# Encoder block on one core: output projection on two scaled fp16 planes, totals and turns beside the score tiles

## The chip, the cores and the metric

The kernel runs on one core of one Trainium2 chip. A core has five engines that the text speaks of: TensorE (PE in the profile, with its weight loads as PEld), VectorE (DVE), ScalarE (ACT), GpSimd (POOL) and SyncE (SP), whose queue issues DMAs. Each works through its own queue in order, and semaphores hold an instruction until its operands are there. The metric is the device time of one execution in microseconds. Three runs of the kernel before gave 1240.5, 1242.0 and 1242.54, median 1242.0.

## What is computed

The reference, cut to its skeleton (one sequence of 1024 tokens, width 1024, 8 neighbourhood heads, 8 window heads on 2 key/value heads, FF width 4096, all float32):

```
h = layer_norm(x, ln0_g, ln0_b)
proj = h @ w_in + b_in
qa, ka, va, qb, kb, vb, ga, gb = split(proj)
y_na = neighbourhood_attention(qa, ka, va, na_rpb) @ w_branch_na
y_swa = windowed_gqa_with_sink(rotary(qb), rotary(kb), vb, sink) @ w_branch_swa
mixed = sigmoid(ga) * y_na + sigmoid(gb) * y_swa
h = layer_norm(ALPHA * h + mixed @ w_out + b_out, ln1_g, ln1_b)
u = square(relu(h @ w_ff1 + b_ff1))
h = layer_norm(ALPHA * h + u @ w_ff2 + b_ff2, ln2_g, ln2_b)
```

## The kernel before

Products are made on split operands: a float32 matrix is held as a high and a low plane, and three matmuls (high·high, high·low, low·high) stand for one. Most products use fp16 planes, scaled by a power of a mean square so that they fit fp16; the scale goes out again when the result is taken from PSUM. The output projection alone uses float32 planes in the matmul's rounded form (fp32r): there is no scale, the planes are a cast and a subtraction.

**Attention** (up to about 400 us) goes in 64 steps, four per head, each with a pair of score tiles: one in the PSUM tag s, one in t (lines 768 to 771). VectorE takes scores out with the bias and the row's extremum (L772), ScalarE makes exponentials, TensorE multiplies with the values (L878). Between these matmuls stand pieces of the input projection (L420), put there by a filler. Some sums with ones (totals over the partitions, for scales of later operands, L193 and the like) and the turned reciprocals of the softmax sums (L828) are made between steps, each in a PSUM tile of tag t of its own. Near the end of attention three additions of 128x2048 (L1074) form a combined operand for the gate products. Gate weights are loaded in steps 24 and on.

**Gate products** follow (to about 465 us); their results go to memory and are read back as sg, the arguments of the sigmoids.

**Branch products** (about 465 to 551 us): for each of 8 column blocks f and 2 halves of the tokens, `branch` makes 12 fp16 matmuls for the neighbourhood branch in tag t and 12 for the window branch in tag o; VectorE takes each out times scale times sigmoid (L1468), and POOL adds the two into mx (L1470). Around them stand per block: the load of a branch weight, its squares on ScalarE (L1360), its product with ones on TensorE (L1365) and its split (L1375, L1376); the load of a row block of w_out and its cast and subtraction (L1458, L1459). The order is written out by hand, engine by engine, in the loop over f and half; a small table B_AT does this for the first blocks during the gate products.

**Output projection** (551 to 646 us): for each of 8 token groups g, `out_mm` makes 2 x 24 matmuls over the column halves (in tags that alternate between mm and s), `split_mx` makes the two planes of the next group's mx, `out_evac` adds the residual (L1560) and takes the statistics (L1563), `ln1_norm` normalises (POOL L1569, ScalarE L275), `turn` transposes the rows of the group before (L1580) in the middle of the group's second half, `turn_evac` scales these into mx (L1591, L1588), and `combine` makes the planes for the first feed-forward product (L1596, L1597). POOL meanwhile prepares the residual rows of later groups (L1732). This order, too, is written by hand. The feed-forward products follow to the end.

## Time and profile before

| what | value |
|---|---|
| median of three runs | 1242.0 us |
| profiled execution | 1243.25 us |
| its span | 1241.5 us |
| TensorE busy | 1216.2 us, 98% |
| VectorE busy | 966.4 us, 78% |
| ScalarE busy | 850.9 us, 69% |
| POOL busy | 333.6 us, 27% |
| mean granted TensorE clock | 0.996 |

A row of the timeline reads: start, duration, engine, line, operation, output and inputs by the program's names, shapes, count of equal instructions in a row, and in brackets how long the engine stood idle before it and for whom. Matmuls overlap in the array, so the time that one takes is read from start to start and not from its duration.

### The profile page before, as it was taken

The page shows a single profiled execution, that of the slowest core. Times are in us where ns is not written, and L with a number is a line of the kernel's source. Part 1 is how long each engine was busy: PE and PEld are TensorE (multiplying, and loading weights), DVE is VectorE, ACT ScalarE, POOL GpSimd, SP SyncE. Part 2 cuts the span into 40 slices and gives each one's busy share as a digit, 9 for nine tenths or more (in the row PEclk, how much of TensorE's full clock was granted, in tenths as well). Part 3 has the DMA queues.
Part 4 walks back from the last instruction along what each step waited for, and adds up shares of the span by engine and source line. Part 5 has one row for each costly group of instructions (what it writes and reads, how often), then busy time and mean ns, then how long its engine had stood idle before and what let it go on. Part 6 is the DMA issues. An engine that isn't in the chain of part 4 may idle for free.

```text
span 1241.5 us, 17090 instructions
## 1 busy us (share of the span) xinstructions
PE 1216.2 (98%) x6050; PEld 638.4 (51%) x6050; DVE 966.4 (78%) x1401; ACT 850.9 (69%) x1369; POOL 333.6 (27%) x358
## 2 busy tenths in 40 slices
PE   8999999999999999999999999999999999999997
PEld 5546565555555444458874444444444444444443
DVE  6788998878876974555788887877767778898898
ACT  7569889998866466533568877788776846344447
POOL 5202222433430013537620031432300001211207
PEclk9999999999999999999999999999999999999998
DMA  8655668686565336645333456776636636363333
GB/s 318 199 183 116 154 155 181 164 186 157 145 135 154 116 119 215 198 152 207 119 136 119 160 191 235 255 245 230 212 118 243 219 136 229 127 261 128 125 111 135
DMA packets 177877, 216.83 MB, mean 175 GB/s; under 512 B 111744, under 2 KB 125312, under 8 KB 171136
## 3 DMA queue, kind: packets, MB, share of 16 engines
q1 hardware_dynamic: 176816, 214.89, 54.5%
q8 instruction: 47, 0.77, 0.3%
q10 hardware_dynamic: 976, 0.87, 0.2%
q14 instruction: 38, 0.31, 0.1%
HBM read 130.69 MB, written 59.33 MB: 153 GB/s over the span
## 4 chain that ended last, share of the span: by engine, by line
PE 78%; ACT 8%; DVE 7%; DMA 2%; issue 2%; POOL 1%; SPq 0%; ACTq 0%; POOLq 0%; DVEq 0%
PE ps_mm L420 16%; PE ps_t L1719 6%; PE ps_o L1719 6%; PE ps_mm L2193 6%; PE ps_s L2193 6%; PE ps_mm L1719 6%; PE ps_t L2193 5%; PE ps_o L2193 5%; PE ps_s L1719 3%; PE ps_o L878 2%; PE ps_o L1162 2%; PE ps_t L1162 1%; PE ps_mm L1162 1%; PE ps_t L410 1%; PE ps_o L410 1%
## 5 line engine op out<-in xcount | busy, mean ns | idle before, releaser
L420 PE MATMUL ps_mm<-hT 128*128 128x512 f16 x960 | 228.1, 381 | 4.9 <-DVE hT L389 2.0
L1719 PEld LDWEIGHTS <-tw 128*128 128x128 f16 x1248 | 122.0, 99 | 146.1 <-issue 1.9
L2193 PEld LDWEIGHTS <-hS 128*128 128x128 f16 x1008 | 98.6, 98 | 118.2
L420 PEld LDWEIGHTS <-hT 128*128 128x128 f16 x960 | 91.0, 100 | 103.7 <-issue 14.4
L791 ACT ACTIVATE ss<-ss,sk 128x384 f32<-128x384 f32 (+1 forms) x128 | 73.9, 578 | 27.9 <-DVE sk L772 27.8
L1719 PE MATMUL ps_t<-hS,tw 128*128 128x512 f16 x384 | 88.1, 379 | 1.5 <-ACT sn L1819 1.1
L1909 DVE TENSOR_TENSOR usl<-usl 128x512 f32<-128x512 f32 x64 | 52.3, 817 | 23.5 <-ACT usl L1837 23.3
L420 PE MATMUL ps_mm<-hT,wpair 128*128 128x512 f16 x288 | 68.7, 380 | 0.0
L1640 POOL TENSOR_TENSOR c<-c 128x2 f32<-128x2 f32 x16 | 15.5, 976 | 193.8 <-DVE c L1639 193.8
L2213 POOL TENSOR_TENSOR acc<-acc,rst 128x512 f32<-128x512 f32 x16 | 32.2, 2012 | 123.6 <-DMA rst<-xr_d 115.7
L200 POOL TENSOR_TENSOR hT<-hT 128x2 f32<-128x2 f32 x30 | 26.4, 880 | 115.7 <-DVE hT L199 115.7
L2026 DVE SCALAR_TENSOR_TENSOR hS<-stg,c,hS 128x2048 f16<-128x2048 f32 x21 | 51.0, 2429 | 7.6 <-ACT hS L2023 7.6
L1646 DVE SCALAR_TENSOR_TENSOR tw<-raw,c,tw 128x512 f16<-128x512 f32 x60 | 51.1, 852 | 4.2 <-ACT tw L1643 3.9
L2193 PEld LDWEIGHTS <-hA 128*128 128x128 f16 x336 | 32.9, 98 | 39.6
L1162 PEld LDWEIGHTS <-hT 128*128 128x128 f16 x336 | 32.9, 98 | 38.8 <-issue 0.3
L878 PE MATMUL ps_o<-pt,vv 128*128 128x256 f16 (+1 forms) x448 | 49.2, 250 | 1.8 <-DMA pt<-hT 1.8
L803 DVE SCALAR_TENSOR_TENSOR pl<-ss,pl 128x768 f16<-128x768 f32 (+1 forms) x42 | 46.7, 1112 | 1.8 <-ACT pl L794 1.6
L1470 POOL TENSOR_TENSOR mx<-sg 128x512 f32<-128x512 f32 x16 | 32.5, 2031 | 51.6 <-DVE sg L1468 51.6
L878 PEld LDWEIGHTS <-vv 128*128 128x128 f16 x448 | 35.5, 98 | 18.8 <-issue 2.1
L1719 PE MATMUL ps_o<-hS,tw 128*128 128x512 f16 x192 | 44.1, 379 | 0.0
L1643 ACT ACTIVATE tw<-raw,c 128x512 f16<-128x512 f32 x60 | 41.7, 709 | 2.8 <-DVE raw L1684 2.8
L2193 PE MATMUL ps_mm<-hA,hS 128*128 128x512 f16 x192 | 42.9, 379 | 0.0
(413 smaller groups left out, 3066.4 us busy)
## 6 DMA issues: line engine op xcount, KB each, us to landing
us_d<-usl SPq DMA_DIRECT2D x112, 256.0 KB, 3.1
stg<-us_d SPq DMA_DIRECT2D x28, 1024.0 KB, 4.8
raw<-in_w_ff SPq DMA_DIRECT2D x24, 512.0 KB, 5.6
sg<-sg_d SPq DMA_DIRECT2D x32, 256.0 KB, 2.9
hA<-in_w_ff SPq DMA_DIRECT2D x8, 1024.0 KB, 7.7
hS<-in_w_ff SPq DMA_DIRECT2D x8, 1024.0 KB, 7.7
hT<-in_w_in SPq DMA_DIRECT2D x60, 128.0 KB, 2.6
hT<-in_w_in SPq DMA_DIRECT2D x11, 512.0 KB, 4.4
```

What stands on the lines that cost most here:

```text
L420: PE.matmul(ps, a[:, k, :], act(b, k), start=(k == 0 and i == 0), stop=(k == NK - 1 and i == 2))
L791: ACT.activation(p, p, AF.Exp, bias=nm[:, i:i + 1], scale=-1.0, accum_out=sums_l[o_chunk][:, hh, 2 * t + i:2 * t + i + 1])
L803: DVE.scalar_tensor_tensor(out=pl[:, n:2 * n], in0=e[:, 0:n], scalar=P_SCALE, in1=pl[:, 0:n], op0=ALU.mult, op1=ALU.subtract)
L878: PE.matmul(o, vs, move(part), start=(m == 0 and part == 0), stop=(m == len(runs) - 1 and part == 1))
L1162: PE.matmul(ps, w[:, a, k, :], act[:, b, k, :], start=(first and k == 0 and m == 0), stop=(k == 3 and m == 2), skip_group_check=True)
L1470: POOL.tensor_tensor(out=mx[:, f, half * 512:(half + 1) * 512], in0=both[0], in1=both[1], op=ALU.add)
L1643: ACT.activation(hi_lo(slot, 0), src, AF.Copy, bias=0.0, scale=w_scale(p))
L1646: DVE.scalar_tensor_tensor(out=hi_lo(slot, 1), in0=src, scalar=w_scale(p), in1=hi_lo(slot, 0), op0=ALU.mult, op1=ALU.subtract)
L1719: PE.matmul(ps, ww, act[:, part, k, :], start=(first and k == 0 and m == 0), stop=(k == 3 and m == 2), skip_group_check=True)
L1909: DVE.tensor_tensor(out=out, in0=a, in1=b, op=op)
L2026: DVE.scalar_tensor_tensor(out=slot[:, :, 1, :], in0=src, scalar=scale, in1=slot[:, :, 0, :], op0=ALU.mult, op1=ALU.subtract)
L2193: PE.matmul(ps, st[:, a, part, j * P:(j + 1) * P], w[:, a, wpart, :], start=(first and a == 0 and m == 0), stop=(a == 3 and m == 2), skip_ ...
```

## The change

Four things are edited.

1. In the attention steps the totals with ones no longer take a tile of tag t. They are written into columns 384 and up of the newest score tile in tag s, which scores never use; the turned reciprocals go to columns 384 to 511 of the score tile in tag t.
2. The three large additions become six of half the size, one a step; the gate loads come two steps later; one small bound is moved from the last steps of attention to the start of the gate products.
3. The output projection works on scaled fp16 planes. Each row block of w_out gets squares (ScalarE), a product with ones (TensorE), a scale (VectorE, POOL) and a scaled split. mx gets squares per block and half, one scale for tokens 0 to 511, made in the middle of the last branch product, and one for tokens 512 to 1023, made behind group 1 of the projection. The result is scaled back in `out_evac`; the scale of w_out's block goes into the branch's own scale.
4. With that, loads, squares and splits of the branch stage change places, and the split of groups 0 and 1 goes behind the last branch product.

```
-                    self.ps = psum("t") if ps is None else ps
+                    self.ps = total_bank() if ps is None else ps
...
+    def total_bank():
+        if not in_steps:
+            return psum("t")
+        c = 384 + 2 * (n_tot[0] % 64)
+        n_tot[0] += 1
+        return score_ps[0][:, c:c + 2]
...
-            ps = psum("t")
+            ps = score_ps[1][:, 384:512]
...
-                if 6 <= H < 13:
-                    g_load(H - 6, i)
+                q = 4 * H + i - 26
+                if 0 <= q < 28:
+                    g_load(q // 4, q % 4)
...
-                        s1_sum(i - 1)
+                elif 0 <= 4 * H + i - 57 < 6:
+                    s1_sum(4 * H + i - 57)
...
+        def wo_square(k):
+            ACT.activation(junkb, wo_raw[k], AF.Square, accum_out=wsq_o[:, k:k + 1], saturate=False)
+        def wo_scale(k):
+            ps, t = psum("s"), wt_o[:, 2 * k:2 * k + 2]
+            PE.matmul(ps[:, 0:2], ones_b, wsq_o[:, k:k + 1].to_broadcast([P, 2]), start=True, stop=True)
+            DVE.scalar_tensor_tensor(out=t, in0=ps[:, 0:2], scalar=Q_MIN, in1=cvb, op0=ALU.max, op1=ALU.mult)
+            w, b = wsc_o[:, 2 * k:2 * k + 2], bsc[:, 4 * k:4 * k + 4]
+            POOL.tensor_tensor(out=w, in0=t, in1=pwb, op=ALU.pow)
+            POOL.tensor_scalar(out=b[:, 2:4], in0=o_back, scalar1=b[:, 1:2], scalar2=w[:, 1:2],
+                               op0=ALU.mult, op1=ALU.mult)
...
-            ACT.copy(wo[:, 0, k, :], wo_raw[k])
-            DVE.tensor_tensor(out=wo[:, 1, k, :], in0=wo_raw[k], in1=b32(wo[:, 0, k, :]), op=ALU.subtract)
+            ACT.activation(wo[:, 0, k, :], wo_raw[k], AF.Copy, bias=0.0, scale=sc)
+            DVE.scalar_tensor_tensor(out=wo[:, 1, k, :], in0=wo_raw[k], scalar=sc, in1=wo[:, 0, k, :],
+                                     op0=ALU.mult, op1=ALU.subtract)
...
+        def mx_square(f, half):
+            j = 8 * half + f
+            ACT.activation(junkm, mx[:, f, half * 512:(half + 1) * 512], AF.Square, accum_out=msq[:, j:j + 1],
+                           saturate=False)
+        def mx_scale(half, ps, ones_, pw_):
+            DVE.tensor_reduce(out=mtot[:, half:half + 1], in_=msq[:, 8 * half:8 * half + 8], axis=mybir.AxisListType.X,
+                              op=ALU.add)
+            PE.matmul(ps[:, 0:2], ones_, mtot[:, half:half + 1].to_broadcast([P, 2]), start=True, stop=True)
...
-            ACT.copy(m[:, 0], mx[:, :, tok(g)])
-            DVE.tensor_tensor(out=m[:, 1], in0=mx[:, :, tok(g)], in1=b32(m[:, 0]), op=ALU.subtract)
+            ACT.activation(m[:, 0], mx[:, :, tok(g)], AF.Copy, bias=0.0, scale=mx_sc(g, 0))
+            DVE.scalar_tensor_tensor(out=m[:, 1], in0=mx[:, :, tok(g)], scalar=mx_sc(g, 0), in1=m[:, 0],
+                                     op0=ALU.mult, op1=ALU.subtract)
...
+                    if f + 1 < 8:
+                        wo_scale(f + 1)
+                        if f:
+                            b_split(f + 1)
...
+                if half == 0:
+                    if f + 1 < 8:
+                        wo_square(f + 1)
+                    if f + 2 < 8:
+                        b_square(f + 2)
+                if f or half:
+                    mx_square(*((f, 0) if half else (f - 1, 1)))
+                branch(f, half, (lambda: mx_scale(0, psum("s"), ones_b, pwb)) if (f, half) == (7, 1) else None)
...
-                if f == 7 and half == 0:
-                    split_mx(0)
-                    split_mx(1)
+        split_mx(0)
+        split_mx(1)
+        mx_square(7, 1)
...
-        DVE.tensor_tensor(out=z[:, ns], in0=pss[g, n], in1=z[:, ns], op=ALU.add)
+        DVE.scalar_tensor_tensor(out=z[:, ns], in0=pss[g, n], scalar=mx_sc(g, 1), in1=z[:, ns],
+                                 op0=ALU.mult, op1=ALU.add)
...
+            if g == 1:
+                mx_scale(1, psum("o"), ones, pw)
```

The queue of TensorE at the change from the first to the second half of branch 0, before: the window product in ps_o, then the next neighbourhood product in ps_t.

```order
L411 LDWEIGHTS wb
L411 MATMUL ps_o<-oS,wb 128x512
L412 LDWEIGHTS wb
L412 MATMUL ps_o<-oS,wb 128x512
L410 LDWEIGHTS wb
L410 MATMUL ps_t<-oS,wb 128x512
L411 LDWEIGHTS wb
```

The same place now (lines 410 to 412 have become 419 to 421):

```order
L420 LDWEIGHTS wb
L420 MATMUL ps_o<-oS,wb 128x512
L421 LDWEIGHTS wb
L421 MATMUL ps_o<-oS,wb 128x512
L1400 MATMUL ps_s<-bc 128x2
L419 LDWEIGHTS wb
L419 MATMUL ps_t<-oS,wb 128x512
```

A product with ones (L1400, of `wo_scale`) has come between the halves; it reads the squares of the next row block of w_out.

The queue of ScalarE from the first sigmoids (L1449) on, before; L1360 are squares of a branch weight, L1458 the cast of w_out's block.

```order
L1375 ACTIVATE wb<-braw,bc 128x1024
L1449 ACT_TABLE_LOAD
L1449 ACTIVATE sg<-sg,prm 128x512 x6
L1360 ACTIVATE bc<-braw 128x1024
L1458 CAST wo<-raw 128x1024
```

And now (sigmoids L1508, split of w_out's block L1409, its squares L1396, squares of the branch weight L1374, squares of mx L1476):

```order
L1388 ACTIVATE wb<-braw,bc 128x1024
L1508 ACT_TABLE_LOAD
L1508 ACTIVATE sg<-sg,prm 128x512 x2
L1409 ACTIVATE wo<-raw,bc 128x1024
L1508 ACTIVATE sg<-sg,prm 128x512 x2
L1396 ACTIVATE bc<-raw 128x1024
L1374 ACTIVATE bc<-braw 128x1024
L1508 ACTIVATE sg<-sg,prm 128x512 x2
```

The branch weight's squares have moved ahead of the third pair of sigmoids, and the squares of w_out's block, which L1400 reads, stand behind the second pair.

VectorE from the last-but-one branch product to the first projection result, before:

```order
L1459 TENSOR_TENSOR wo<-raw,wo 128x1024
L1468 SCALAR_TENSOR_TENSOR sg<-ps_t,bc,sg 128x512
L1468 SCALAR_TENSOR_TENSOR sg<-ps_o,bc,sg 128x512
L1437 TENSOR_TENSOR m<-mx,m 128x1024 x2
L1468 SCALAR_TENSOR_TENSOR sg<-ps_t,bc,sg 128x512
L1468 SCALAR_TENSOR_TENSOR sg<-ps_o,bc,sg 128x512
L1459 TENSOR_TENSOR wo<-raw,wo 128x1024
L1560 TENSOR_TENSOR z<-ps_mm,z 128x512
```

And now (L1521 takes out a branch product, L1480 and L1484 belong to `mx_scale`, L1495 is the low plane, L1619 the projection's result):

```order
L1521 SCALAR_TENSOR_TENSOR sg<-ps_t,bc,sg 128x512
L1521 SCALAR_TENSOR_TENSOR sg<-ps_o,bc,sg 128x512
L1480 TENSOR_REDUCE prm<-prm 128x1
L1484 TENSOR_SCALAR mxc<-ps_s 128x2
L1521 SCALAR_TENSOR_TENSOR sg<-ps_t,bc,sg 128x512
L1521 SCALAR_TENSOR_TENSOR sg<-ps_o,bc,sg 128x512
L1495 SCALAR_TENSOR_TENSOR m<-mx,mxc,m 128x1024 x2
L1619 SCALAR_TENSOR_TENSOR z<-ps_mm,mxc,z 128x512
```

The low planes of groups 0 and 1 stood ahead of the last branch product's two results and now stand behind both; the sum for the scale stands ahead of them.

## The prediction

> **What bounds the kernel now.** I read the page first, then the chain of waits of TensorE, then the windows and the timeline of the stages that the change touches.

> ```profile
> PE 1216.2 (98%) x6050; PEld 638.4 (51%) x6050; DVE 966.4 (78%) x1401; ACT 850.9 (69%) x1369; POOL 333.6 (27%) x358
> ```

> TensorE is busy 98% of the span; all its idle time is about 25 us. So the change can gain in three ways: shorter matmuls, idle gaps that close, or a clock that is not lowered. It loses wherever a matmul is put in TensorE's queue ahead of work that was ready, with an operand that comes late. The waits of TensorE, with total, count and longest, show the gaps that this change touches:

> ```profile
> PE ps_s L1365 <- ACT bc L1360: 2.1, 1, 2.1
> PE ps_t L770 <- DVE sk L772: 1.6, 3, 1.0
> PE ps_mm L420 <- DVE hT L256: 0.9, 2, 0.7
> PE ps_t L770 <- ACT rt L830: 0.7, 1, 0.7
> PE ps_t L1580 <- ACT z L275: 0.2, 1, 0.2
> ```

> Attention owns the second to fourth, the start of the branch products the first, and the end of the output projection the last. In the projection itself TensorE hardly waits.

> **Attention: totals and turns beside the score tiles.** The gaps at L770 are waits for a free ps_t tile, which the totals with ones (L193) and the turned reciprocals (L828) also took. With those in the score tiles, this wait goes. But a total written into the ps_s score tile must wait until VectorE has evacuated that tile (L772), which it did not before. TensorE, then VectorE, around 141 us:

> ```profile
> 140.74 0.28 PE L193 MATMUL ps_t<-hT 128*128 128x2 f32 x2
> 142.59 0.44 PE L770 MATMUL ps_t<-kh,q 128*128 128x384 f32 x1 [0.33 <-DVE sk L772]
> ```
> ```profile
> 141.37 0.61 DVE L772 CUSTOM_DVE_ANT_0 ss<-ps_s,bd,snk 128x384 f32<-128x384 f32 x1
> ```

> The total stood at 140.74; now it waits for the evacuation to end at 141.98, so everything behind it moves 1.24 us, while the wait at 142.59 (0.33 idle, some 0.48 by starts) goes: +0.76. The step at 173 has the same picture (its total some 1.25 before the evacuation's end): together +1.5. One step gains, since its wait for the evacuated reciprocal goes, −0.75:

> ```profile
> 191.08 0.44 PE L770 MATMUL ps_t<-kh,q 128*128 128x384 f32 x1 [0.75 <-ACT rt L830]
> ```

> Around 358 VectorE is late because of a 2.54-us addition, which the change halves. VectorE, TensorE, and the windows of the stage (the last three columns are the granted clock, the share of the DMA engines and GB/s):

> ```profile
> 356.29 2.54 DVE L1074 TENSOR_TENSOR g<-hT 128x2048 f32<-128x2048 f16 x1
> ```
> ```profile
> 359.83 0.38 PE L770 MATMUL ps_t<-kh,q 128*128 128x256 f32 x1 [0.98 <-DVE sk L772]
> 361.03 4.17 PE L420 MATMUL ps_mm<-hT 128*128 128x512 f16 x11 [0.70 <-DVE hT L256]
> ```
> ```profile
> 360.00:362.00 2.00, 1.30 (x5) 0.55 (x6) 2.00 (x4) 1.94 (x5) 0.01 (x1) 0.73 0.43 153
> 362.00:364.00 2.00, 2.00 (x7) 0.62 (x6) 2.00 (x1) 1.27 (x2) 2.00 (x1) 0.50 0.52 119
> ```

> Two gaps of 0.98 and 0.70 are followed by half clock (0.50), in which 11 matmuls take 4.17 us. With an addition of some 1.27 in place of 2.54 the evacuation comes 1.27 earlier and both gaps nearly close; I leave 0.4 for totals that now wait there: −1.3. If the gaps go, so does the low clock: the 11 matmuls take 11 × 0.216 = 2.4 (0.216 is shown below) instead of 4.1 from start to start, −1.7. Sum of attention: +1.5 − 0.75 − 1.3 − 1.7 = **−2.25**. Unknown is at how many further steps the total now waits; bounds: −3.75 if the two steps cost nothing, 0 if the low clock stays or three more steps cost 0.76. The gate loads, two steps later, lie on the SP queue behind the same neighbours and have steps to spare: 0.

> **Start of the branch products.** TensorE, then ScalarE:

> ```profile
> 470.06 0.38 PE L410 MATMUL ps_t<-oS,wb 128*128 128x512 f16 x1
> ```
> ```profile
> 471.67 1.96 ACT L1449 ACTIVATE sg<-sg,prm 128x512 f32<-128x512 f32 x3 [1.27 <-DMA sg<-sg_d]
> 476.33 1.04 ACT L1360 ACTIVATE bc<-braw 128x1024 fp8e5<-128x1024 f32 x1
> 477.28 0.18 ACT L1360 ACTIVATION_READ_ACCUMULATOR bc<-braw 128x1 f32 x1
> ```

> Before, the squares of a branch weight (L1360) stood behind six sigmoids that wait for DMA, and TensorE waited 2.1 for them, some 2.2 by starts. Now these squares come after only two late sigmoids, and that wait goes. But the product with ones that scales the next output weight stands ahead of the second half of branch 0, ready at 470.06. Its squares (like L1360, 1.04 + 0.18) stand behind two sigmoids whose data land at 471.67: 471.67 + 2 × 0.65 + 1.2 = 474.2. TensorE waits 4.15 instead of 2.2: **+1.95**. VectorE, POOL and the evacuation queue behind it with slack.

> The trace shows what idle time can do to the clock: 1.7 us of it in two gaps was followed by half clock, worth 1.7. A gap of 4.15 in one piece I expect to bring the same: **+1.75**. Against it stands this window, in which a gap of 2.1 left the clock at 1.00:

> ```profile
> 476.00:478.00 2.00, 0.48 (x4) 0.37 (x5) 0.25 (x1) 2.00 (x4) 1.27 (x1) 1.00 0.36 137
> ```

> The bounds are 0 and 2.4.

> Later branches: per f ScalarE has four sigmoids, two splits, two squares of 1024 and two of 512, worked out from these groups as 4 × 0.67 + 2 × 1.15 + 2 × 1.23 + 2 × 0.87 = 9.2 (a 512 square costed like a sigmoid plus its read), within 48 matmuls of 0.216 = 10.4:

> ```profile
> L1449 ACT ACTIVATE sg<-sg,prm 128x512 f32<-128x512 f32 x16 | 10.9, 716 | 10.3 <-DMA sg<-sg_d 10.2
> L1375 ACT ACTIVATE wb<-braw,bc 128x1024 f16<-128x1024 f32 x7 | 8.0, 1148 | 7.4 <-POOL bc L1368 7.4
> ```

> It fits: 0, at most +1.5 where a load is late.

> **End of the branch products and output projection.** POOL, TensorE and VectorE:

> ```profile
> 546.81 1.27 POOL L1470 TENSOR_TENSOR mx<-sg 128x512 f32<-128x512 f32 x1 [3.01 <-DVE sg L1468]
> 548.37 0.38 PE L410 MATMUL ps_o<-oS,wb 128*128 128x512 f16 x1
> 550.31 0.38 PE L410 MATMUL ps_o<-oS,wb 128*128 128x512 f16 x1
> 550.74 0.38 PE L412 MATMUL ps_o<-oS,wb 128*128 128x512 f16 x1
> 551.42 0.39 PE L1553 MATMUL ps_mm<-wo,m 128*128 128x512 f32 x1
> ```

> The scale of the activations needs a sum in the middle of the last branch: the addition ends at 548.08, ScalarE squares 0.87, VectorE reduces some 0.2, so the product with ones starts at about 549.3 where TensorE would go on at 548.37: +0.95. Then the low plane of the first group stands on VectorE behind the evacuation of the last branch tile: 550.74 + 0.95 + 0.43 to the evacuation, 0.67, and a low plane of 1.28 (as L1376):

> ```profile
> 467.88 1.28 DVE L1376 SCALAR_TENSOR_TENSOR wb<-braw,bc,wb 128x1024 f16<-128x1024 f32 x1
> ```

> That gives 554.1 for the third matmul of the projection, which stood at 551.42: +2.7.

> fp16 itself gains. Nine fp16 matmuls take 550.31 − 548.37 = 1.94, 0.216 each; nine of the projection 576.19 − 574.15 = 2.04, 0.227 each:

> ```profile
> 574.15 0.39 PE L1552 MATMUL ps_mm<-wo,m 128*128 128x512 f32 x1
> 576.19 0.39 PE L1552 MATMUL ps_mm<-wo,m 128*128 128x512 f32 x1
> ```

> For 384 matmuls that is −4.3. By the end of group 1 it has given back 94 × 0.011 = 1.0, which leaves +1.65. There the second scale stands ahead of group 2, behind VectorE's work on group 1, which is ready only at 575.97:

> ```profile
> 575.82 0.15 DVE L1568 TENSOR_SCALAR mv<-mv 128x1 f32<-128x1 f32 x1
> 576.96 8.29 POOL L1732 TENSOR_TENSOR zl<-zl 128x512 f32<-128x512 f32 x5
> 590.15 1.25 ACT L275 ACTIVATE zl<-zl,mv 128x1024 f32<-128x1024 f32 x1 [3.32 <-POOL mv L273]
> ```
> ```profile
> L1368 POOL TENSOR_TENSOR bc<-bc 128x2 f32<-128x2 f32 x6 | 4.2, 708 | 2.2 <-DVE bc L1366 2.2
> ```

> With a reduction of 0.2 (the small operation here takes 0.15) TensorE stands some 2.2 more. But from here TensorE is not alone on the path: POOL runs without a gap from 576.96 to the normalisation at 590.15, and its new power (0.7, as the last row, a group of the branch products) goes ahead of that. So z of group 2 comes at +1.65 + 0.7 = +2.4. From then VectorE, POOL and ScalarE go round in a loop:

> ```profile
> 591.93 3.06 DVE L1597 TENSOR_TENSOR hA<-mx,hA 128x512 f16<-128x512 f32 x2 [4.08 <-ACT hA L1596]
> 603.82 3.05 DVE L1597 TENSOR_TENSOR hA<-mx,hA 128x512 f16<-128x512 f32 x2 [2.88 <-ACT hA L1596]
> 640.40 1.23 ACT L275 ACTIVATE z<-z,mv 128x1024 f32<-128x1024 f32 x1
> 641.68 1.09 PE L1580 MATMUL ps_t<-ident,z 128*128 128x128 f32 x8
> ```

> ```profile
> L1468 DVE SCALAR_TENSOR_TENSOR sg<-ps_t,bc,sg 128x512 f32<-128x512 f32 x15 | 11.3, 751 | 12.0 <-PE ps_t L412 5.6 <-issue 4.9 <-POOL bc L1368 0.9
> 599.11 0.68 DVE L1560 TENSOR_TENSOR zl<-ps_s,zl 128x512 f32<-128x512 f32 x1
> ```

> A round takes 11.89, and VectorE's only gap in it, 2.88, waits on ScalarE, not on TensorE. Scaled evacuations (0.75 for 0.68, twice, by the rows here) and low planes (1.28 above, at most 0.05 over a subtraction of that size) add some 0.17 a round, five times. At group 6 z ends at 641.63 and the turn starts at 641.68: no slack. So the end comes at 2.4 + 0.85 = **+3.25** against before, and TensorE spends its saving waiting for turns. Bounds: 2.7 + 2.2 − 4.3 = +0.6 if TensorE alone sets the pace, and +4.

> **Sum.** −2.25 + 1.95 + 1.75 + 3.25 = +4.7. The profiled execution took 1243.25, span 1241.5; the changed one would take 1247.95. It stood 1.25 above the median of 1242.0, so the median becomes 1246.7. A measurement tells 0.2%, 2.5 us, from no change.

> **Rivals.**
> - The clock stays up at the branch start: +2.95, 1245.0. [...] By the trace, gaps of 1.7 in pieces were enough once, and 2.1 not enough once. Chance 0.15.
> - The loop of VectorE, POOL and ScalarE doesn't bind: the turns find their rows ready, the end comes at +0.6 instead of +3.25: +2.05, 1244.05. For it: only 0.2 us of waiting at L1580 is seen. Against: the turn at 641.68 has no slack. Chance 0.20.
> - Not slower: the fp16 saving of 4.3 arrives whole, because the sums for the scales and the first low plane are ready in time at both ends of the projection. −2.25 + 3.7 − 4.3 = −2.85, 1239.15. It decides if VectorE's reductions are done before TensorE gets to the product, which needs some 0.95 and 2.2 that I do not see. That fp16 runs no faster here speaks against this too, but the rows above have it at 0.216. Chance 0.13.
> - Attention costs more: totals wait 0.76 at six more steps, +4.5 on top, 1251.2. Against: VectorE mostly evacuates well before the total. Chance 0.12.

> **The numbers.** My forecast has 0.40, mostly within 1.5 of 1246.7. Slower: 0.36 of it, 0.09 of the first rival, 0.04 of the second, all 0.12 of the last: 0.61. Within 0.2%: 0.04 + 0.06 + 0.14 = 0.24. Faster: 0.02 of the second and 0.13 of the third: 0.15. The range from 1239.5 to 1250.5 leaves out most of the third and the last.

> **What would show it.** Right: a TensorE wait of about 4 us near 470 behind squares on ScalarE, then half clock; waits near 549, at the third projection matmul, and before group 2; matmuls 0.216 apart in the projection; turns waiting for z of groups 5 to 7; 0.98 and 0.70 near 360 gone. Wrong: sigmoid data that land earlier than 4 us after their issue, a round of the loop that shrinks under 11.4, or totals that wait at many steps.

## The result, and the profile after

The changed kernel took 1251.36 us (median; 1251.06 to 1251.82), before 1241.76; ratio 1.0079, 95% interval 1.0061 to 1.0096. It is slower by 9.6 us. The forecast was slower, 1246.7 with a range to 1250.5: the sign was right, the size half of what came, and the measured time lies 0.9 beyond the range.

The profiled execution took 1251.06, span 1249.2. Its page, and TensorE's waits (total, times, longest):

```profile
PE 1215.4 (97%) x6070; PEld 607.5 (49%) x6070; DVE 970.9 (78%) x1416; ACT 870.9 (70%) x1417; POOL 339.2 (27%) x368
```
```profile
PE ps_s L1400 <- ACT bc L1396: 4.3, 1, 4.3
PE ps_s L193 <- DVE sk L781: 2.8, 3, 1.2
PE ps_t L1640 <- ACT z L284: 2.1, 1, 2.1
PE ps_o L1482 <- DVE prm L1480: 2.1, 1, 2.1
...
PE ps_mm L1612 <- DVE m L1495: 1.6, 1, 1.6
...
PE ps_mm L1174 <- DVE go L1249: 0.8, 1, 0.8
...
PE ps_s L1482 <- DVE prm L1480: 0.5, 1, 0.5
```

TensorE is as busy as before (1215.4 for 1216.2), though the projection's matmuls are shorter: what they save went into 20 more matmul instructions for the products with ones (6070 for 6050) and into matmuls at a lower clock. Each wait that the forecast named is there: the squares of w_out (4.3), the totals in the score tile (2.8), the turn (2.1, of group 6 alone), the second scale (2.1), the first low plane (1.6) and the first scale (0.5). The one in the gate products (0.8) was not named.

Set side by side, the same matmul in both profiles starts later by so much (worked out from the two timelines, before to after; the place is the matmul's start in before, and the first row includes 0.8 for the bound that was moved there):

| place | shift of starts | change in the stage | forecast for the stage |
|---|---|---|---|
| end of attention (397.06) | −2.54 | −2.54 | −2.25 |
| end of gate products (459.70) | −1.57 | +0.97 | 0 |
| end of branch block 1 (487.90) | +3.96 | +5.53 | +3.7 |
| first projection matmul (550.77) | +5.78 | +1.82 | +0.95 |
| first matmul of group 2 (573.92) | +8.62 | +2.84 | +2.9 |
| first feed-forward matmul (645.81) | +8.97 | +0.35 | −0.6 |
| last matmul | +7.78 | −1.19 | 0 |

The stage that missed most is the third. Its windows (last columns: granted clock, DMA share, GB/s):

```profile
468.00:470.00 2.00, 0.80 (x4) 0.18 (x2) 0.00 (x0) 1.73 (x3) 0.00 (x0) 1.00 0.75 218
470.00:472.00 2.00, 0.00 (x0) 0.00 (x0) 1.22 (x2) 2.00 (x4) 0.00 (x0) 1.00 0.95 299
472.00:474.00 2.00, 0.94 (x4) 0.66 (x5) 1.54 (x4) 1.97 (x3) 0.48 (x1) 0.57 0.78 301
474.00:476.00 2.00, 2.00 (x6) 0.65 (x5) 0.00 (x0) 2.00 (x7) 1.78 (x3) 0.50 0.22 25
476.00:478.00 2.00, 2.00 (x6) 0.76 (x5) 0.00 (x0) 1.53 (x3) 0.00 (x0) 0.50 0.89 326
478.00:480.00 2.00, 2.00 (x8) 0.81 (x7) 0.75 (x1) 0.94 (x2) 0.00 (x0) 0.72 0.49 186
```

TensorE stands from 468.6 to 473.1. The clock is at half for 2 × 2 × (0.43 + 0.50 + 0.50 + 0.28) = 6.8 us, from 472.3 on. In the first 0.8 of that TensorE still stood, so what it lost is half of the other 6.0: 3.0, where the forecast had priced 1.75. ScalarE shows why TensorE stood: sigmoids, the squares of w_out's block, then TensorE may go.

```profile
470.65 1.32 ACT L1508 ACTIVATE sg<-sg,prm 128x512 f32<-128x512 f32 x2
471.88 1.04 ACT L1396 ACTIVATE bc<-raw 128x1024 fp8e5<-128x1024 f32 x1
472.82 0.19 ACT L1396 ACTIVATION_READ_ACCUMULATOR bc<-raw 128x1 f32 x1
```

In the projection TensorE's queue reads as forecast: the third matmul waits for the low plane, group 2 for the second scale, the turn of group 6 for its rows.

```profile
558.75 0.39 PE L1612 MATMUL ps_mm<-wo,m 128*128 128x512 f16 x1 [1.61 <-DVE m L1495]
...
582.29 0.38 PE L1482 MATMUL ps_o<-prm,c 128*128 128x2 f32 x2 [2.07 <-DVE prm L1480]
...
649.24 1.50 PE L1640 MATMUL ps_t<-ident,z 128*128 128x128 f32 x8 [2.08 <-ACT z L284]
```

Behind that last wait the clock is at half once more, from 649.78 for 3.4 us (its row stands in the last section). The forecast had no such term. The first feed-forward matmul comes 6.81 after the normalisation of group 6 has started (647.97), where it takes 5.16 in e2, e4 and e6, whose profiles lack a low clock there: 1.65 for the clock, inside the row +0.35.

And the normalisations on ScalarE keep their round, 608.89 to 620.79, 11.90 us, as 11.89 before, although each group has 0.5 us less of matmuls:

```profile
608.89 1.25 ACT L284 ACTIVATE zl<-zl,mv 128x1024 f32<-128x1024 f32 x1 [2.62 <-POOL mv L282]
620.79 1.24 ACT L284 ACTIVATE zl<-zl,mv 128x1024 f32<-128x1024 f32 x1 [5.18 <-POOL mv L282]
```

### The profile page after: what moved, and what is told of

The parts are those of the page before. It is cut to its first block, busy times and chain, and to the rows that moved or that the text cites. A ratio compares the mean times of both kernels' runs of the same rounds, so it can differ in the third digit from the quotient of the medians.

```text
span 1249.2 us, 17241 instructions
## 1 busy us (share of the span) xinstructions
PE 1215.4 (97%) x6070; PEld 607.5 (49%) x6070; DVE 970.9 (78%) x1416; ACT 870.9 (70%) x1417; POOL 339.2 (27%) x368
## 4 chain that ended last, share of the span: by engine, by line
PE 82%; ACT 7%; DVE 6%; issue 2%; DMA 2%; POOL 1%; POOLq 0%; SPq 0%; ACTq 0%; DVEq 0%
PE ps_mm L429 17%; PE ps_t L1779 6%; PE ps_o L1779 6%; PE ps_mm L2255 6%; PE ps_s L2255 6%; PE ps_mm L1779 6%; PE ps_t L2255 5%; PE ps_o L2255 5%; PE ps_s L1779 2%; PE ps_o L887 2%; PE ps_o L1174 2%; PE ps_mm L1174 1%; PE ps_t L1174 1%; PE ps_t L419 1%; PE ps_o L419 1%
## 5 line engine op out<-in xcount | busy, mean ns | idle before, releaser
L1523 POOL TENSOR_TENSOR mx<-sg 128x512 f32<-128x512 f32 x16 | 30.1, 1881 | 49.8 <-DVE sg L1521 23.8
L587 POOL TENSOR_TENSOR bm<-tb,mk 128x128 f32<-128x128 f32 x56 | 42.9, 796 | 0.7
```

Of the source, the lines that this page charges most:

```text
L587: bias_ops.append(lambda o=o, g0=g0, m=m, g=g: POOL.tensor_tensor(out=bm[:, o + g * P:o + (g + 1) * P].rearrange("p (a c) -> p a c", c=8), ...
```

## The experiments

The theory after the result: the opening of the branch stage costs a wait and a low clock behind it; in the projection the loop of VectorE, POOL and ScalarE sets the end, so that fp16 saves nothing there; the attention edit is no gain on the median. The rivals stand with each run. Medians in us, before on the same chip beside them:

| run | median | before | ratio, 95% interval |
|---|---|---|---|
| e1 squares early | 1251.5 | 1242.6 | 1.0064 (1.0040 to 1.0088) |
| e2 filler | 1250.56 | 1242.6 | 1.0069 (1.0053 to 1.0084) |
| e3 second scale early | 1252.2 | 1242.6 | 1.0085 (1.0066 to 1.0103) |
| e4 low plane first | 1251.44 | 1242.6 | 1.0075 (1.0057 to 1.0093) |
| e5 before again | 1242.13 | 1240.95 | one run |
| e6 plain fp16 | 1239.3 | 1240.95 | 0.9981 (0.9971 to 0.9991) |
| e7 plain fp16, loads early | 1236.87 | 1240.95 | 0.9966 (0.9953 to 0.9978) |
| e8 attention only | 1241.19 | 1240.95 | 0.9999 (0.9989 to 1.0009) |
| e9 w_out's steps later | 1248.31 | 1241.2 | 1.0063 (1.0048 to 1.0078) |
| e10 all mended | 1244.16 | 1241.2 | 1.0028 (1.0018 to 1.0039) |
| e11 before, loads early | 1238.83 | 1241.2 | 0.9985 (0.9975 to 0.9994) |
| e12 best parts | 1234.78 | 1240.41 | 0.9954 (0.9940 to 0.9968) |

**e1: the squares of the second block of w_out early.**

```
-  10: ((b_scale, 1),)}
+  10: ((b_scale, 1), (wo_square, 1))}
...
-                    if f + 1 < 8:
+                    if 0 < f < 7:
                         wo_square(f + 1)
```

> The squares of the second row block of w_out are made during the gate products, ahead of the sigmoids; nothing else differs from the changed kernel (1251.4). Theory (late squares make the wait of 4.43 us, and that idle time brings the low clock, worth 3.1): both go, -7.5, 1244 to 1245, clock 1.00 from 470 to 480. Rival (the sigmoids' data are late anyway and TensorE waits for them next): a wait of over 2 us stays near 470 to 475, at most -4, 1247 or more.

The rival had the time right, and its wait came at another place. The wait at the opening is gone, but a wait of the same kind comes up one block later (the larger of the two):

```profile
PE ps_s L1400 <- ACT bc L1396: 4.6, 2, 3.3
```
```profile
483.44 1.06 ACT L1396 ACTIVATE bc<-raw 128x1024 fp8e5<-128x1024 f32 x1 [1.94 <-DMA raw<-in_w_out]
```

Here it is not the sigmoids' data that are late, as the rival said, but the load of the third block, which SP issues at 478.18, behind sigmoid loads that it issues from 477.29 on. Where one late step was mended, the next late one took its place, with 6.8 us at half clock behind it again (from 483.95). One of the four executions took 1247.29, at a mean clock of 0.998; the other three had 0.994 to 0.995 and took 1251.38 to 1254.6.

**e2: filler in the gap.**

```
             ps, t = psum("s"), wt_o[:, 2 * k:2 * k + 2]
+            for _ in range(18 if k == 1 else 0):
+                PE.matmul(ps, bws[0][0][:, 0, :], o_na(0, 0, 0), start=True, stop=True)
```

> The changed kernel with 18 extra fp16 matmuls, whose results are overwritten, ahead of the product with ones that waits at the start of the branch products: 3.9 us of work in a wait of 4.43. Theory (idle time lowers the clock): the wait falls under 0.8, the clock stays at 1.00, and the time falls by about 3.1 although work is added: 1248.3. Rival (the slow matmuls there have another cause, such as the DMA traffic of the loads): clock 0.5 again, time 1251 to 1252.

With eighteen useless matmuls the clock stays at 1.00 in the gap:

```profile
472.00:474.00 2.00, 2.00 (x11) 0.93 (x10) 0.10 (x1) 2.00 (x4) 0.00 (x0) 1.00 0.94 294
474.00:476.00 2.00, 1.16 (x6) 0.31 (x4) 2.00 (x3) 2.00 (x3) 0.00 (x0) 1.00 1.04 375
476.00:478.00 2.00, 1.71 (x9) 0.93 (x10) 0.66 (x2) 1.97 (x6) 1.37 (x2) 1.00 0.20 82
```

From the end of the gate products to the end of block 0, by the starts, the stage costs +5.56 against before instead of +7.76, 2.2 less, with 3.9 us of work added: 1.3 of waiting is left, where 0.5 was planned. DMA traffic is as heavy (0.94 to 1.04 of the engines, 0.95 in the changed kernel from 470 to 472) and the clock stays at 1.00 all the same: this profile fits the theory's idle time and not the rival's traffic. The 3.1 that the expectation had did not come: on the median little is seen (1250.56, ratio 1.0069 for 1.0079, intervals that overlap); this profile also has a wait of 1.9 by starts in attention, near 324, that the changed kernel's own lacks, so the 2.2 rest on the stage's rows alone.

**e3: the second scale early, e4: the low plane early.** In e3:

```
             out_mm(g, 0, 0, 8)
+            if g == 1:
+                mx_scale(1, psum("o"), ones, pw)
...
-            if g == 1:
-                mx_scale(1, psum("o"), ones, pw)
```

> The scale of tokens 512 to 1023 is made behind the first half of group 1 instead of behind all of it. The wait of 2.2 us ahead of group 2 goes. Theory (from group 2 on the loop of POOL, VectorE and ScalarE sets the end, TensorE only waits): only POOL's 0.7 at the normalisation of group 2 can be won, 0 to -0.8, 1250.6 to 1251.4; the wait of TensorE at the turn of group 6 grows by up to 2. Rival (TensorE sets the pace): -2.2, 1249.1.

And e4:

```
+        def first_scale():
+            mx_scale(0, psum("s"), ones_b, pwb)
+            split_mx(0)
...
-        split_mx(0)
         split_mx(1)
```

> The planes of group 0 are made right behind the first scale, ahead of the last branch product's evacuations on VectorE. The wait of 1.77 at the third projection matmul goes. Theory (groups 0 and 1 are paced by TensorE, so the loop starts earlier): -1.2 to -1.8 at the end as well, 1249.6 to 1250.2. Rival (evacuations pushed back delay the last addition and the residual work on POOL, so the loop starts no earlier): 0, 1251.4.

In e3 the wait ahead of group 2 is gone, and TensorE begins that group 2.3 us earlier in relation to the start of the projection. By the first feed-forward matmul 1.6 of it is given back and 0.7 is left, POOL's part as the theory had it; the median shows neither. Its waits at the turns grew, and it waits a second time for a low plane:

```profile
PE ps_t L1640 <- ACT z L284: 2.4, 2, 2.0
PE ps_mm L1612 <- DVE m L1495: 2.1, 2, 1.6
```

e4 is the same: its wait at the third matmul fell from 1.77 to 0.66 by starts, and the turns took it back. There my expectation of −1.2 or more failed. The profile had the clock at half behind the 2.1-us wait ahead of group 2, a wait that in the changed kernel's own profile left it at 1.00; that one had its half clock behind the turn instead. So how much e4 wins by itself is not settled.

```profile
582.00:584.00 2.00, 2.00 (x7) 0.88 (x8) 0.16 (x1) 1.35 (x2) 1.90 (x4) 0.50 0.04 8
```

**e5: the kernel before once more**, without an edit.

> The kernel before, unchanged, profiled once more. Theory (the low clock at 361 to 364 in the first profile comes and goes between executions, so its 1.7 us were no gain to be had on the median): this profile has the two gaps of 0.98 and 0.70 near 360 again, but in about every second execution a clock of 1.00 there and a span about 1.7 shorter, 1239.8. Rival (the gaps always lower the clock): PEclk 0.5 between 361 and 364 again, span 1241.5.

The gaps near 360 are there again, though the first is shorter (0.72 and 0.69 idle, for 0.98 and 0.70); the clock is not lowered:

```profile
360.00:362.00 2.00, 1.03 (x5) 0.60 (x6) 2.00 (x4) 1.94 (x6) 0.00 (x0) 1.00 0.74 249
362.00:364.00 2.00, 2.00 (x11) 0.89 (x10) 2.00 (x3) 1.71 (x2) 1.57 (x1) 1.00 0.24 56
```

The span is 1240.3 for 1241.5. So the low clock at 361 comes in some executions only; two profiles don't tell in how many. The mean clocks give a hint: of the 22 executions of before on this chip, six have 0.996, as the first profile had, with a median of 1242.75, and twelve have 0.998, with a median of 1240.29. Where in those executions the clock was low is not recorded.

**e6: fp16 without scales.**

```
-        wo = r1p.tile([P, 2, NK, D], F32R, tag="r1", name="wo")
+        wo = r1p.tile([P, 2, NK, D], F16, tag="r1", name="wo")
...
-            m = xps[g % 2].tile([P, 2, 8, P], F32R, tag="m", name="m")
+            m = xps[g % 2].tile([P, 2, 8, P], F16, tag="m", name="m")
...
```

> The kernel before with fp16 planes for w_out and mx in place of fp32r, made as before by a cast and a subtraction: no squares, no scales, no moved step (it leaves out the scaling that keeps any input in fp16's range). Theory (from group 2 on the loop of POOL, VectorE and ScalarE sets the end of the projection): TensorE saves 4.3 in matmuls but waits at the turns of groups 5 to 7; 0 to -1.2 in all, 1240.4 to 1241.6. Rival (TensorE sets the pace): -4.3, 1237.3.

It wins 0.19% (0.09 to 0.29%), 1.65 us by the medians: more than the theory's 1.2 and less than half of the rival's 4.3. TensorE waits at the turns instead (0.2 before):

```profile
PE ps_t L1580 <- ACT z L275: 2.1, 3, 1.4
```

**e7: the same, and the last weight loads in the middle of group 5.**

```
                 turn(g - 1)
+            if g == 5:
+                op_places("S1", "S2")
+                for p in range(2, 4):
+                    head_w(p)
```

(The same calls later in group 5 are taken out.)

> As the kernel with plain fp16 planes, and the loads of the last two feed-forward weight pieces (2 x 1 MB into hS, on SP's queue behind the store of group 5) are issued in the middle of group 5, some 8 us earlier. Theory (ScalarE makes their squares ahead of the normalisation of group 6, so that load is a link of the loop): the normalisation of group 6 comes 2.8 us earlier, and -2.5 to -4 in all, 1237.6 to 1239. Rival (VectorE's own round is the link): no more than the plain planes alone, 1240.4 to 1241.6.

It is 2.4 under e6 (six of its seven executions lie under nine of e6's ten) and 4.1 under before, a little more than the expected 2.5 to 4. ScalarE in e6 and then in e7; in e6 the squares (L1629) wait for DMA and hold the normalisation (L275) behind them, in e7 they are done before POOL gives the word:

```profile
621.23 1.24 ACT L275 ACTIVATE z<-z,mv 128x1024 f32<-128x1024 f32 x1 [4.61 <-POOL mv L273]
...
632.19 1.91 ACT L1629 ACTIVATE junk<-hS 128x2048 fp8e5<-128x2048 f32 x1 [1.83 <-DMA hS<-in_w_ff]
634.00 0.19 ACT L1629 ACTIVATION_READ_ACCUMULATOR junk<-hS 128x1 f32 x1
634.10 1.23 ACT L275 ACTIVATE z<-z,mv 128x1024 f32<-128x1024 f32 x1
```
```profile
623.26 1.24 ACT L275 ACTIVATE z<-z,mv 128x1024 f32<-128x1024 f32 x1 [4.60 <-POOL mv L273]
...
630.50 1.91 ACT L1629 ACTIVATE junk<-hS 128x2048 fp8e5<-128x2048 f32 x1
632.32 0.19 ACT L1629 ACTIVATION_READ_ACCUMULATOR junk<-hS 128x1 f32 x1
633.29 1.24 ACT L275 ACTIVATE z<-z,mv 128x1024 f32<-128x1024 f32 x1 [0.79 <-POOL mv L273]
```

From group 5 to group 6 it is 12.87 in e6 and 10.03 in e7, so the load is a link of the loop. In the two profiles 1.6 of the gain lies ahead of the first feed-forward matmul and 1.2 behind it.

**e8: the attention edit alone**, the diff's first two points on the kernel before.

> The kernel before with the attention part of the change alone: totals and turns beside the score tiles, halved additions, gate loads two steps later, the bound moved. Theory (two waits of 1.4 for the evacuation of the score tile, one more at 206, and what is won at 360 is partly given back at the gate products, where VectorE is late): -0.5 to +0.5 against the median of before, 1241.3 to 1242.3; against an execution with a low clock at 361, -1.5. Rival (my forecast): -2.25, 1239.5.

Ratio 0.9999: nothing, as the theory said, but not for the reason given. No wait in the gate products follows, so VectorE's lateness there, which I had put down to the attention edit, comes with the branch edit's steps that stand among the gate products. What eats the gain of 1.7 at 360 and 0.75 at 190 is seen in the waits: the totals, and a DMA wait that was 1.8 before. Behind that DMA wait this profile, the slowest of the ten executions (1243.59), also has 3.4 us at half clock, so it lost more than the median did. Two of its waits, and that stretch (granted clock third from the end):

```profile
PE ps_o L887 <- DMA pt<-hT: 2.5, 1, 2.5
PE ps_s L193 <- DVE sk L781: 2.1, 3, 1.2
```
```profile
214.05:217.46 3.41, 3.41 (x12) 2.01 (x10) 3.10 (x7) 3.37 (x8) 3.41 (x7) 0.50 0.83 215
```

**e9: all steps of w_out half a block later.**

```
                 if half == 0:
-                    wo_split(f)
+                    if f:
+                        if f + 1 < 8:
+                            wo_load(f + 1)
+                        wo_scale(f)
...
                 else:
-                    if f + 2 < 8:
-                        wo_load(f + 2)
-                    if f + 1 < 8:
-                        wo_scale(f + 1)
-                        if f:
-                            b_split(f + 1)
+                    if f == 0:
+                        wo_square(1)
+                    wo_split(f)
+                    if f and f + 1 < 8:
+                        b_split(f + 1)
...
```

(The squares of later blocks move to the second half as well.)

> The changed kernel, with the steps for w_out's row blocks (load, squares, product with ones, split) each put half a block later in the branch stage, so that the load and the squares have a half more before TensorE needs them. Theory (the wait of 4.4 us at the opening and the low clock behind it, 3.1, are what the branch stage costs; the wait of the first attempt came back only because the next load was late): a wait under 1.5 at the opening and no low clock there in most executions, 1244 to 1246. What stays over before: the projection's end, about 3, and 0.9 for eight more products with ones. Rival (another load or square steps into the gap): a wait over 3 somewhere between 468 and 500 and a time of 1249 or more.

The waits for w_out's squares fell from 4.3 to 2.1 in two pieces, none over 1.2, the clock stayed at 1.00, and the stage up to the end of block 1 went from +5.53 to −0.53 against before (the second of the two waits comes just behind it). But it missed its time, 1248.31 for 1244 to 1246: up to the projection it gave back 2.8, of which 1.1 is the second of these waits and 1.05 the first scale's, 1.6 for 0.5; the other 0.6 is not traced.

```profile
PE ps_s L1400 <- ACT bc L1396: 2.1, 2, 1.2
...
PE ps_s L1482 <- DVE prm L1480: 1.6, 1, 1.6
```

By the rows, VectorE begins the low plane of w_out's last block at 547.44, 0.17 ahead of POOL's addition of the half that the scale is taken from, and the addition takes 2.23; in the changed kernel the same addition began at 551.46 beside an idle VectorE and took 1.26. The first scale comes later by that. VectorE and POOL of e9:

```profile
547.44 1.28 DVE L1410 SCALAR_TENSOR_TENSOR wo<-raw,bc,wo 128x1024 f16<-128x1024 f32 x1
```
```profile
547.61 2.23 POOL L1523 TENSOR_TENSOR mx<-sg 128x512 f32<-128x512 f32 x1 [3.01 <-DVE sg L1521]
```

**e10: e9 with e3, e4 and the early loads.**

> As the kernel with w_out's steps later, and also: the second scale behind the first half of group 1, the planes of group 0 ahead of the last evacuations, and the loads of the last two feed-forward weight pieces in the middle of group 5. Theory (the loop sets the end; its links are the start of group 0, POOL's power at group 2 and the late loads): 1.5 + 0.7 + 2.5 less than that kernel, 1239 to 1241.5, below before. Rival (TensorE's own waits set the end): 2.2 + 1.1 less, 1241 to 1243.

It took 4.1 less than e9, about the 4.7 of the theory; but as e9 had missed, it ends at 1244.16, still slower than before. From the first projection matmul to the first feed-forward one it takes 2.5 less than before, where the changed kernel took 3.2 more, 1.65 of it the low clock behind the turn. Three things were mended at once, so the share of e3 and e4 in this is not shown. What remains against before lies ahead of the projection: the 0.8 in the gate products, a wait of 2.4 for squares, the first scale's 1.6, and the steps' own matmuls.

**e11: the kernel before with the early loads.**

> The kernel before with only the loads of the last two feed-forward weight pieces issued in the middle of group 5. Theory (with fp32r the loop and TensorE are level, the turn of group 6 has no slack on either side, so a shorter loop alone brings little): 0 to -0.8 against before. Rival (the loop alone set the end before too): -2.4 as on the plain fp16 planes.

The rival had the size right, −2.4 or −0.15%, but not its reason: up to the first feed-forward matmul nothing is won (−0.08 against before, so loop and TensorE were level there). The feed-forward products' own waits at their start, 1.1 and 0.4 in before, go but for 0.3. That they hang on the same squares is argued from the code and not tried by itself.

**e12: the best parts together:** e7, with halved additions and turned reciprocals beside the score tile, and totals as before.

> Plain fp16 planes and the early loads (1236.9), with the two parts of the attention edit that remove a wait: halved additions and turned reciprocals beside the score tile; totals stay in tiles of their own. Theory (the totals' waits of 1.4 ate what the other two parts won, and VectorE's lateness at the gate products gives back 0.8 to 1): waits of 1.4 at 141 and 173 absent, those at 190 and 360 gone, -0.5 to -1.5 against 1236.9, 1235.4 to 1236.4. Rival (attention is paced by loads and VectorE as a whole, so single waits don't add up): 1236.9.

At 1234.78 it beats both kernels, the one before by 0.46% (0.32 to 0.60%), and it lies 0.6 below the expected range; like e6 and e7 it leaves out the scales that keep any input in fp16's range. The gaps of 0.98 and 0.70 near 360 are gone; the wait at 190 is not, against my expectation:

```profile
PE ps_t L771 <- ACT rt L831: 0.7, 1, 0.7
...
PE ps_t L771 <- DVE sk L773: 0.7, 2, 0.3
```

Its interval overlaps that of e7, which ran on another chip, so the gain of 2.1 between the medians is not shown as e12's own.

## Why the prediction was right or wrong

**Attention, −2.25.** In the two profiles it was −2.54, with totals waiting at 141 and 173 as worked out. But 1.7 of it was the step "If the gaps go, so does the low clock", and e5 shows an execution of before without that low clock. A term was taken from one execution's clock; the edit alone is worth nothing on the median (e8).

**Opening, +1.95 for the wait.** 4.3 of idle time was measured against 4.15 forecast; the place held, and so did the mechanism, squares that stand behind late sigmoids (e1, e9). In detail the late data were those of the first pair of sigmoids (landed at 468.2), not of the second; from there on ScalarE had work without a wait.

**Its clock, +1.75: the mis-sized term.** The step "A gap of 4.15 in one piece I expect to bring the same" failed: it took the price of one spell at half clock, 1.7, for a gap that brought two. The spell lasted 6.8 us and cost 3.0 of TensorE's time. The one near 361 lost at least 2 × (0.27 + 0.50) = 1.54 by its two rows; by the trace it lasted 3.41 us, from 360.93 to 364.34, and the one at the opening 6.83, from 472.29 to 479.12: the second is two of the first. Ahead of the opening's spell no matmul ran from 468.88 to 472.29; ahead of the one at the turn TensorE was busy for 1.33 of the 3.41 us, and half clock followed there too. The rival that kept the clock up was wrong here.

**The clock behind the turn, a term put at nothing.** "TensorE spends its saving waiting for turns" gave that wait no price beyond itself. In the profile it is followed by a second spell at half clock, 1.65 us.

**Later branches, 0.** They cost 0.87 beyond the first scale. ScalarE did fit; but the eight more products with ones are themselves work of TensorE, some 0.14 each, which the sum left out.

**Gate products, 0.** +0.97, most of it the wait of 0.8, from the branch edit's steps that now stand there (e8 lacks it). By the rows it is the squares of w_out's first block: ScalarE makes them at 447.15, VectorE stands 1.0 for ScalarE's next result until 449.36, and from there on it has no gap up to the result at 457.34 that TensorE waits for. This was not tried by itself.

**End of the branches and projection, +3.25.** Measured +0.95, +2.84 and +0.35, less 1.19 that the feed-forward products' start gives back: 2.95. That the total came close is in part luck. The row +0.35 holds 1.65 of half clock that the sum did not have, and "some 0.17 a round" for slower work on VectorE did not come: from group 2 to group 5 the rounds took 11.91, 11.90 and 13.63, before 11.89, 11.87 and 13.61 (starts of the normalisations on ScalarE). The loop as what holds TensorE there is shown by e3 and e6: removed waits of TensorE come back at the turns, and fp16 alone wins less than half of 4.3. The forecast's loop left out one thing, that the link between groups 5 and 6 is a load: shortening it wins 2.4 in e7. But e11 wins as much with nothing won ahead of the feed-forward products, so how much of the 2.4 the loop gave is open.

**From profile to median.** The step "It stood 1.25 above the median … so the median becomes 1246.7" failed: the changed kernel's profile stands 0.3 under its median. In the profiles the difference is 7.8, in the medians 9.6. Part of the 1.25 was probably the low clock at 361 that the sum had counted as a gain already, so it was taken off twice (the 22 executions at e5 speak for it; the spell itself was seen in one profile).

**Together.** The sum had −1.7 and +1.75 for the clock, next to nothing. An estimate from the rows above: on the median the gain of 1.7 is not there, the opening costs 1.3 more than forecast and the turn 1.65, 4.6 in all, of the 4.9 by which the forecast fell short; the other misses nearly cancel. The other three executions of the changed kernel have mean clocks of 0.994 to 0.995, as the profiled one has 0.994, so a loss of this size seems the rule there; where it lies in them is not recorded.

## What to carry to other kernels

Before an edit that puts a small matmul into a full queue is called free, follow its operand back to the slowest load; moving it earlier only helps if the next block's load has room too. A shorter matmul pays only where TensorE sets the pace (in e6 an estimated saving of 4.3 us brought 1.65): compare the round of the other engines with that of the matmuls first, and shorten the round's own links (here a load that could start some 6 us earlier in its round: in e6 it is issued 1.6 behind the normalisation of group 5, in e7 4.6 ahead of it). Behind a wait the clock cost nearly as much again in some places and nothing in others: 3.0 us behind the 4.3 of the opening and 1.65 behind the 2.1 of the turn, none behind the 2.1 ahead of group 2 (all in the changed kernel's profile). So a wait of that size should be priced with that and without. A gain that a clock's state makes should be looked for in a second profile before it enters a sum, and then not be taken off again as the distance to the median.

## What the runs showed of the hardware

```profile
578.10:581.51 3.41, 2.12 (x10) 0.78 (x8) 2.03 (x4) 1.40 (x5) 2.62 (x3) 1.00 0.05 19
581.51:584.92 3.41, 2.62 (x14) 1.32 (x15) 0.82 (x5) 1.70 (x3) 2.56 (x4) 1.00 0.02 5
646.37:649.78 3.41, 1.33 (x9) 0.72 (x8) 0.05 (x1) 3.41 (x5) 0.00 (x0) 1.00 0.00 0
649.78:653.19 3.41, 3.41 (x15) 2.17 (x13) 3.41 (x6) 3.41 (x9) 0.00 (x0) 0.50 0.37 154
```

In e4 the gap ahead of group 2 lies whole in one stretch, and half clock follows:

```profile
578.27:581.68 3.41, 1.38 (x7) 0.41 (x5) 2.40 (x7) 0.66 (x2) 1.88 (x3) 1.00 0.50 211
581.68:585.09 3.41, 3.37 (x9) 1.46 (x10) 0.82 (x3) 2.44 (x4) 3.23 (x5) 0.50 0.13 52
```

The busy time in the stretch ahead does not by itself tell when: in before 1.83 us of it from 357.52 to 360.93 was followed by 0.50, and 1.65 from 207.33 to 210.74 by 1.00. In e2, with useless matmuls in the gap, the clock stayed at 1.00 at a DMA share of 0.94 to 1.04. And an addition of 128x512 on POOL (L1470 in before, L1523 in e9) took 2.23 us in e9 with a VectorE operation that began 0.17 before it. In before 13 of the 16 begin 0.16 to 0.17 behind such an operation of 128x1024 and take 2.17 to 2.24, and the other three, with VectorE idle, take 1.27. So POOL's result came 2.23 us behind its addition's start in e9 and 1.26 behind it at the same place in the changed kernel, without any wait between them.
